# One DiT layer on one core: LayerNorm 1 and the first FFN products by token tiles, block 3 of the output projection folded into the residual in two parts, gate sums loaded behind the conditioning

## The chip, the cores and the metric

The kernel runs on one core of a Trainium2 chip. The metric is the device time of one execution in microseconds (us); smaller is better. The engines are TensorE (PE in the profile, its weight loads PEld), VectorE (DVE), ScalarE (ACT), GpSimd (POOL) and SyncE (SP), which issues the DMA transfers. All weights are read from HBM once.

## The reference

One layer of a diffusion transformer, batch 1: 256 latent tokens `x` and 256 context tokens `ctx` of width D = 2048, and a conditioning vector `c`. All in float32.

```python
m = silu(c) @ w_ada + b_ada                # 6 modulations of width D: shift, scale, gate; shift, scale, gate
u = x * (1 + scale1) + shift1              # the context likewise, with its own vector
q, k, v = split(u @ w_in)                  # 16 query heads of 128, in two groups with 2 key heads each
o = attention(q, k, v)                     # group A: window of 128, sink; group B: RMS-normalised q, k; both rotary
x = layer_norm1(alpha * x + gate1 * (o @ w_out))
u2 = x * (1 + scale2) + shift2
h = silu(u2 @ w_gate) * (u2 @ w_up)        # hidden width 5632
x = layer_norm2(alpha * x + gate2 * (h @ w_down))
```

Each layer norm has its own weight and bias over the width.

## The kernel before

**Products.** The 256 latent tokens are two token tiles (`t`) of 128, one tile on the 128 partitions. A float32 product is made of three passes on PE in a faster format: each operand is split into `hi`, a rounded copy, and `lo`, the rest, and `mm3` (L221 to L223) adds hi by hi, hi by lo, and lo by hi into one accumulator bank `acc` of 128x512. Weights come in raw tiles of 1 MB (4 by 128 rows, 512 columns) into the rooms `raw` (4) and `araw` (2); ACT copies `hi` and DVE subtracts to get `lo`, two of 128x1024 for each raw tile (L439 and L442 while the planner below works, L211 and L212 in the FFN). A raw tile feeds 24 products, 12 for each token tile.

**Order.** Up to the first layer norm each piece of work is a step (engine, estimated duration, what it follows, rooms it takes and gives back, a due time `F.at`) of a planner, `Flow`. `Flow.run` goes through time with these estimates: on each engine the step that is ready and due first is started, and the instructions are written out in the order in which the steps started. The estimates set the order; on the chip each engine works its list through in that order, waiting where it must. SP's list of loads is made in the same way, so a load that has to wait for a room holds up those behind it. After `F.run()` the order is that of the program text.

**Stages.** 1. Conditioning columns: w_ada for the first modulation, products on PE (L476). 2. `u` and the combined projection w_in. 3. Attention in four groups of heads `gi`: scores, row maxima on DVE (L814), exponentials on ACT (L826), transposes of the probabilities on PE (L844), products with the values (L855). 4. The output projection: four blocks `n` of 512 columns, each in two halves: head groups 0 and 1 are multiplied during attention and the partial sums kept in `outacc`; head groups 2 and 3 follow after attention (`flow_out((2, 3), n, n == 3)`). Block 3 goes by token tiles: all products of tile 0, then all of tile 1. DVE adds the halves (L1020), multiplies by the gate (L1024), adds alpha times x into `xt` (L1025) and takes the statistics (L1026), per tile. 5. Layer norm 1, its scalars on DVE for each tile (`ln_scalars`, L959 to L969) and `normalise` (L976) for each of four blocks of columns; its weight and bias and the second modulation are folded into columns `mA` and `mB`. `z_part(kk)` transposes two blocks of 128 columns of `xt` for both tiles (L1215); ACT applies `mA` and `mB` (`uf`, L1219) and rounds (`u2h`, L1221), DVE subtracts (`u2l`, L1222). 6. The FFN by hidden blocks `f` of 512 columns, gate and up products, then w_down, then layer norm 2.

**Sums on DVE.** Three modulations are not computed on PE: w_ada tiles are multiplied by the conditioning and summed on DVE (`flow_vector`, L329): gate 1 into `g1b` (16 loads of 1 MB), then the first block of the second shift and scale into `adav`. When the gate's sums are there, PE adds over the partitions and spreads to all rows (`rows_of_gate`, L339, four blocks of 512); the columns of the second modulation are made likewise (`m0_columns`, L908). A second block of shifts is summed on PE (`m1_sums`, L1161), copied by ACT (`m1_copy`) and placed as columns (L1177, L1180). The rest of the second modulation (`scales`, `side`) is summed on DVE between the first FFN products.

**Spills.** As the second modulation isn't complete when the FFN starts, the first `SPLIT_F` hidden blocks are begun with the first k-groups of u2 (one group for the first `ONE_F` = 3 blocks, two for the others); ACT copies the partial sums to `spill` (L1280) and DVE adds them later.

**Warm-up.** `warm` issues small products whose results nobody reads (L1038): 8 before the first flips and 6 between the two `z_part`.

## Time and profile before

| | us |
|---|---|
| three runs | 1183.93, 1187.5, 1189.0 (median 1187.5) |
| profiled execution | 1195.69 |
| its span | 1193.9 |
| PE busy | 1159.9 (97%) |
| DVE busy | 817.2 (68%) |
| ACT busy | 531.3 (45%) |
| mean granted clock of PE | 0.988 |
| moved by DMA | 292.95 MB, mean 245 GB/s |

The profile's page gives for each engine the time in which it had an instruction, and its share of the span. A matmul of 128x512 is put down with 0.39 us, but one starts every 0.23 us where nothing is waited for, since they overlap; so idle time of PE is where none is in flight. A granted clock of 0.5 means that PE ran at half speed there. The three runs are of the same kernel without the profiler.

### The profile page before, as it was taken

To read this page: it belongs to the slowest core of one execution; us is meant where nothing else is said; L and a number is where in the kernel's file an instruction comes from. 1 tells how busy PE (TensorE), PEld (TensorE's weight loads), DVE (VectorE), ACT (ScalarE), POOL (GpSimd) and SP (SyncE) were. 2 spreads that over 40 slices of the span, in tenths; PEclk is the share of its full clock that TensorE was granted. 3 is DMA by queue.
4 is the path that set the end of the run, shared out by engine and by line. 5 is a ranking of instruction groups with operands and counts; after the bars stand their busy time and mean duration, and the time that the engine had idled before them with its cause. 6 is when DMAs were issued, how large, how long until landed. Compare 5 with 4: busy or idle time off the path is not lost.

```text
span 1193.9 us, 14384 instructions
## 1 busy us (share of the span) xinstructions
PE 1159.9 (97%) x5591; PEld 937.1 (78%) x5591; DVE 817.2 (68%) x1052; ACT 531.3 (45%) x746; POOL 24.4 (2%) x44
## 2 busy tenths in 40 slices
PE   8999899999999999999999999999999999999994
PEld 8766578787878877788888888888888888888883
DVE  4653479989887888777676566564545768676556
ACT  3331352677666245444644444444444434343340
POOL 1000200000000000010000000000000000000000
PEclk9989999999999989999999999999999999999997
DMA  8998996634677369999776565556565889777531
GB/s 275 374 382 313 383 396 240 219 112 153 233 250 245 106 240 340 351 333 337 262 216 210 181 197 186 177 185 203 177 198 191 315 312 317 289 258 247 207 133 71
DMA packets 150716, 292.95 MB, mean 245 GB/s; under 512 B 5580, under 2 KB 20332, under 8 KB 148343
## 3 DMA queue, kind: packets, MB, share of 16 engines
q1 hardware_dynamic: 150648, 292.04, 70.5%
q8 instruction: 44, 0.72, 0.2%
q14 instruction: 24, 0.20, 0.0%
HBM read 289.92 MB, written 2.10 MB: 245 GB/s over the span
## 4 chain that ended last, share of the span: by engine, by line
PE 80%; DVE 8%; DMA 8%; ACT 2%; issue 1%; POOL 0%; SPq 0%; DVEq 0%; ACTq 0%; POOLq 0%
PE acc L222 23%; PE acc L223 23%; PE acc L221 23%; DMA raw<-in_w_ada_dram 3%; DMA raw<-in_w_in_dram 3%; DVE adav L329 2%; PE wk L855 2%; DVE lo L212 1%; PE wk L476 1%; PE acc L1038 1%; DMA lgb<-in_ln_b_dram 1%; PE wk L1259 1%; PE wk L844 1%; PE wk L339 1%; DMA raw<-in_w_gate_dram 1%
## 5 line engine op out<-in xcount | busy, mean ns | idle before, releaser
L212 DVE TENSOR_TENSOR lo<-raw,hi 128x1024 fp32r<-128x1024 f32 x262 | 317.8, 1223 | 215.3 <-ACT hi L211 211.7
L211 ACT CAST hi<-raw 128x1024 fp32r<-128x1024 f32 x262 | 273.5, 1053 | 363.8 <-PE acc L223 306.9
L222 PE MATMUL acc<-lo,u2h 128*128 128x512 f32 x704 | 275.6, 391 | 1.6 <-DVE lo L212 1.6
L221 PE MATMUL acc<-hi,u2h 128*128 128x512 f32 x704 | 274.3, 392 | 1.1 <-ACT hi L211 1.1
L223 PE MATMUL acc<-hi,u2l 128*128 128x512 f32 x704 | 274.6, 390 | 0.0
L222 PEld LDWEIGHTS acc<-lo,u2h 128*128 128x128 f32 x704 | 132.6, 188 | 31.7 <-DVE lo L212 4.7
L221 PEld LDWEIGHTS acc<-hi,u2h 128*128 128x128 f32 x704 | 132.5, 188 | 28.5 <-ACT hi L211 1.5
L223 PEld LDWEIGHTS acc<-hi,u2l 128*128 128x128 f32 x704 | 132.5, 188 | 27.4
L439 ACT CAST hi<-raw 128x1024 fp32r<-128x1024 f32 (+1 forms) x82 | 83.6, 1030 | 143.3 <-PE acc L223 74.7
L221 PE MATMUL acc<-hi,hTh 128*128 128x512 f32 x344 | 135.5, 394 | 0.0
L223 PE MATMUL acc<-hi,hTl 128*128 128x512 f32 x344 | 134.0, 390 | 0.0
L222 PE MATMUL acc<-lo,hTh 128*128 128x512 f32 x344 | 134.0, 390 | 0.0
L329 DVE SCALAR_TENSOR_TENSOR adav<-raw,cs,adav 128x512 f32<-128x512 f32 (+1 forms) x128 | 121.4, 948 | 13.2 <-DMA raw<-in_w_ada_dram 11.0
L442 DVE TENSOR_TENSOR lo<-raw,hi 128x1024 fp32r<-128x1024 f32 (+1 forms) x82 | 97.5, 1195 | 37.0 <-ACT hi L439 36.7
L221 PE MATMUL acc<-hi,uh 128*128 128x512 f32 x256 | 103.8, 406 | 2.7 <-ACT hi L439 2.6
L222 PE MATMUL acc<-lo,uh 128*128 128x512 f32 x256 | 101.1, 395 | 2.8 <-DVE lo L442 2.8
L223 PE MATMUL acc<-hi,ul 128*128 128x512 f32 x256 | 100.5, 393 | 0.0
L222 PEld LDWEIGHTS acc<-lo,hTh 128*128 128x128 f32 x344 | 64.6, 188 | 14.3 <-issue 1.0
L221 PEld LDWEIGHTS acc<-hi,hTh 128*128 128x128 f32 x344 | 64.6, 188 | 14.3 <-issue 1.0
L223 PEld LDWEIGHTS acc<-hi,hTl 128*128 128x128 f32 x344 | 64.6, 188 | 13.2
L221 PEld LDWEIGHTS acc<-hi,uh 128*128 128x128 f32 x256 | 48.4, 189 | 20.0 <-ACT hi L439 6.2
L222 PEld LDWEIGHTS acc<-lo,uh 128*128 128x128 f32 x256 | 48.6, 190 | 13.6 <-DVE lo L442 4.4
(193 smaller groups left out, 1167.3 us busy)
## 6 DMA issues: line engine op xcount, KB each, us to landing
raw<-in_w_ada_dram SPq DMA_DIRECT2D x72, 1024.0 KB, 7.5
raw<-in_w_gate_dram SPq DMA_DIRECT2D x44, 1024.0 KB, 5.7
raw<-in_w_up_dram SPq DMA_DIRECT2D x44, 1024.0 KB, 5.2
raw<-in_w_down_dram SPq DMA_DIRECT2D x44, 1024.0 KB, 5.3
raw<-in_w_ada_dram SPq DMA_DIRECT2D x48, 512.0 KB, 5.8
raw<-in_w_in_dram SPq DMA_DIRECT2D x18, 1024.0 KB, 8.6
raw<-in_w_out_dram SPq DMA_DIRECT2D x16, 1024.0 KB, 5.0
raw<-in_w_in_dram SPq DMA_DIRECT2D x10, 512.0 KB, 7.5
```

The source lines that it names most:

```text
L211: nc.scalar.copy(hi[:, :n], raw[:, s : s + n])
L212: nc.vector.tensor_tensor(lo[:, :n], raw[:, s : s + n], hi[:, :n].bitcast(F32), op=ALU.subtract)
L221: nc.tensor.matmul(ps, lhsT=xh, rhs=w[0], start=first, stop=False)
L222: nc.tensor.matmul(ps, lhsT=xh, rhs=w[1], start=False, stop=False)
L223: nc.tensor.matmul(ps, lhsT=xl, rhs=w[0], start=False, stop=last)
L329: nc.vector.scalar_tensor_tensor(a[:, c : c + piece], raw[:, f : f + piece], cs[:, g * (G4 * NB // w) + j, 2:3], a[:, c : c + piece], op0= ...
L339: nc.tensor.matmul(ps, lhsT=ones, rhs=sb[:, s : s + NB], start=True, stop=True)
L439: nc.scalar.copy(hl.hi[:, :n], raw.t[:, s : s + n])
L442: nc.vector.tensor_tensor(hl.lo[:, :n], raw.t[:, s : s + n], hl.hi[:, :n].bitcast(F32), op=ALU.subtract)
L476: nc.tensor.matmul(bank.t[32 * j : 32 * j + 32, :width], lhsT=cs[:, k, 2 - 2 * i : 34 - 2 * i], rhs=raw.t[:, c * width : (c + 1) * width], ...
L844: nc.tensor.transpose(ps.t[:, k * P : (k + 1) * P], probs[i].t[:, k * P : (k + 1) * P], ident)
L855: nc.tensor.matmul(o_ps.t[:, : 2 * P], lhsT=v, rhs=pT.t[:, k].rearrange("p h q -> p (h q)"), start=k == 0, stop=k == 3)
```

## The change

1. **Loads.** A step `start` without duration on SP follows the last conditioning load of stage 1; the constants' loads (`const_loads`: rotary tables, norm weights, sinks), the gate sums' bias and their 16 loads wait for it in the plan. In the plan a `raw` or `araw` room comes back 1300 ns after its last reader (`AGAIN`) instead of 90 to 270.
2. **Gate rows and columns.** The steps `rows_of_gate`, `ln_flip` and `m0_columns` are planned 2.5 us behind their sums (`SLACK`), and the loads of the gate's sums are spread until END + 10 instead of END - 15, END being the planned end of attention.
3. **Block 3 of the output projection.** Its `hi` and `lo` take rooms of another pool (`spare`: `b4`) and are loaded 14 us earlier; the rooms `hl` are so free for the first w_gate and w_up tiles, whose loads and casts become steps of the plan (`first_gate`, `first_up`). `finish` is now single steps: for block 3 the half in `outacc` is multiplied by the gate and added to alpha times x before the products end; behind them come gate (L1035), last addition (L1041) and statistics (L1044).
4. **m1 sums.** Their loads may use `araw` too and are due 35 us earlier; `m1_copy` moves behind the first products.
5. **Layer norm 1 by token tiles.** The plan ends with the scalars and flips of tile 0 (`z_flip`, L1233). Then the program goes: `z_rest` of tile 0, scalars of tile 1, gate products of tile 0, flips of tile 1, up products of tile 0, `z_rest` of tile 1, both products of tile 1, spills. The 14 warm-up products are gone.
6. **Spills.** `SPLIT_F` is 10 instead of 8.

```diff
-SPLIT_F = 8
+SPLIT_F = 10
+SLACK = 2500
+AHEAD = 14
+    AGAIN = 1300
...
-                            heapq.heappush(back, (end + self.OTHER[e], b.pool))
+                            heapq.heappush(back, (end + (self.AGAIN if b.pool.endswith("raw") else self.OTHER[e]), b.pool))
...
-        last = F.add("SP", 500 * len(starts), lambda: first_bias(a, starts, width), [last])
+        last = F.add("SP", 500 * len(starts), lambda: first_bias(a, starts, width), [last, start])
...
-            ld = F.add("SP", dma_ns(P * G4 * NB * 4, 2048), load, take=[room])
+            ld = F.add("SP", dma_ns(P * G4 * NB * 4, 2048), load, [start], take=[room])
...
+            if gs[-1] < 3:
+                outs[n, t] = steps([ends[t], outs[n, t]], add, give=[ps])
+            elif by_tile:
+                at, F.at = F.at, F.at - 6
+                early = steps([outs[n, t], gates[n]], lambda: gate(lambda: outacc[n, t]), base)
+                F.at = at
+                outs[n, t] = steps([ends[t], early], lambda: gate(lambda: ps.t), last, spread, give=[ps])
+            else:
+                a = steps([ends[t], outs[n, t]], add, give=[ps])
+                outs[n, t] = steps([a, gates[n]], lambda: gate(lambda: outacc[n, t]), base, spread)
...
-    a = F.add("SP", 2500, const_loads)
+    a = F.add("SP", 2500, const_loads, [start])
...
-            a = F.add("PE", 900, fn, [last_sum], [room])
+            a = F.add("PE", 900, fn, [(last_sum, -SLACK)], [room])
...
-    gates = rows_of_gate(flow_vector((2 * D,), D, g1b, (gate_from, END - 15)))
+    gates = rows_of_gate(flow_vector((2 * D,), D, g1b, (gate_from, END + 10)))
...
-        F.at = END + 60
-        raw, ld = flow_load(w_ada, g * 4, 4, 3 * D + NB, NB, W)
+        F.at = END + 25
+        raw, ld = flow_load(w_ada, g * 4, 4, 3 * D + NB, NB)
+        ld.after, ld.left = [(m0_sum, 2400)], 1
+        F.at = END + 45
...
-    for t in range(NT):
-        F.add("DVE", 3300, lambda t=t: scalars(t), [outs[n, t] for n in range(4)])
+    first_gate = flow_weights(w_gate, 0, G4, 0, NB, W)
+    first_up = flow_weights(w_up, 0, G4, 0, NB, W)
+    F.at = END + 33
+    a = F.add("DVE", 3300, lambda: scalars(0), [outs[n, 0] for n in range(4)])
+    zroom = [Buf("wk"), Buf("wk")]
+    for i in range(2):
+        F.add("PE", 210, lambda i=i: z_flip(0, 2 * i), [a], [zroom[i]])
     F.run()
...
-    z_part(0)
-    warm(wps, 6)
-    z_part(2)
+    for kk in (0, 2):
+        z_rest(0, kk)
+    scalars(1)
+    first_products(0, 0)
+    for kk in (0, 2):
+        z_flip(1, kk)
+    first_products(1, 0)
+    for kk in (0, 2):
+        z_rest(1, kk)
+    adav1 = vector_sums(NB)
+    nc.scalar.copy(adav1, bank1.t)
+    for i in range(2):
+        first_products(i, 1)
+    for i in range(2):
+        for t in range(NT):
+            nc.scalar.copy(spills[0][i][:, t, :], firsts[i][t])
```

The lines move by 3 to 40: L221 to L223 are L224 to L226 in the changed kernel, L329 is L332, L339 L342, L442 L449, L908 L918, L959 to L969 are L969 to L979, L976 L986, L1161 L1200. What stands where, before and now, at three places:

**SP's loads around the constants.** Before (g1b's bias and the five loads behind it are the constants' group):

```order
L421 DMA raw<-in_w_ada_dram 128x4x512 x6
L542 DMA cxt<-in_ctx_dram 128x2x512
L312 DMA g1b<-in_b_ada_dram 1x2048
L367 DMA cosA<-in_rope_cos_dram 128x2x128
L368 DMA sinA<-in_rope_sin_dram 128x2x128
L369 DMA gq<-in_q_norm_g_dram 128x128
L370 DMA gk<-in_k_norm_g_dram 128x128
L371 DMA sinkb<-in_sink_logit_dram 128x8
L421 DMA raw<-in_w_in_dram 128x4x512
```

Now, behind the last of the conditioning loads (L424 from in_w_ada_dram), with the first gate loads (L322) next:

```order
L424 DMA raw<-in_w_ada_dram 128x4x512 x2
L424 DMA raw<-in_w_in_dram 128x4x512 x3
L315 DMA g1b<-in_b_ada_dram 1x2048
L370 DMA cosA<-in_rope_cos_dram 128x2x128
L371 DMA sinA<-in_rope_sin_dram 128x2x128
L372 DMA gq<-in_q_norm_g_dram 128x128
L373 DMA gk<-in_k_norm_g_dram 128x128
L374 DMA sinkb<-in_sink_logit_dram 128x8
L322 DMA raw<-in_w_ada_dram 128x2048 x2
```

The six small loads went behind four more w_ada loads and five more w_in loads.

**PE's gate rows.** Before, late in attention, two of the four among output products and these two between the flips of the probabilities:

```order
L223 MATMUL acc_3219<-hi_3078,oTl_2479 128x512
L844 MATMUL wk_3266<-ident_70,pr_3227 128x128 x4
L844 MATMUL wk_3273<-ident_70,pr_3230 128x128 x4
L339 MATMUL wk_3280<-g1b_131,ones_98 128x512
L339 MATMUL wk_3287<-g1b_131,ones_98 128x512
L855 MATMUL wk_3292<-pT_3278,kvacc_129 128x256 x2
L855 MATMUL wk_3292<-pT_3278,kvacc_130 128x256 x2
```

Now, behind the second half of block 0 (its last product is the first row) and ahead of block 1's (oTh_2874 is head group 2):

```order
L226 MATMUL acc_3321<-hi_3274,oTl_3163 128x512
L342 MATMUL wk_3441<-g1b_131,ones_98 128x512
L342 MATMUL wk_3447<-g1b_131,ones_98 128x512
L342 MATMUL wk_3453<-g1b_131,ones_98 128x512
L342 MATMUL wk_3457<-g1b_131,ones_98 128x512
L224 MATMUL acc_3461<-hi_3351,oTh_2874 128x512
```

All four moved out of attention, and the 144 products of blocks 1 to 3 stand behind them.

**The transition into the FFN, on PE and DVE.** PE before, from the last output product:

```order
L223 MATMUL acc<-hi,oTl 128x512
L1161 MATMUL wk<-raw,cs 32x512 x16
L1038 MATMUL acc<-ident 128x128 x8
L1215 MATMUL wk<-ident,xt 128x128 x4
L1038 MATMUL acc<-ident 128x128 x6
L1215 MATMUL wk<-ident,xt 128x128 x4
L1177 MATMUL wk<-sel,adav 128x4 x4
L221 MATMUL acc<-hi,u2h 128x512
```

PE now; twelve products of tile 0 and then tile 1's four flips (L1233) follow the first of the FFN:

```order
L226 MATMUL acc<-hi,oTl 128x512
L1200 MATMUL wk<-raw,cs 32x512 x16
L1233 MATMUL wk<-ident,xt 128x128 x4
L224 MATMUL acc<-hi,u2h 128x512
L225 MATMUL acc<-lo,u2h 128x512
L226 MATMUL acc<-hi,u2l 128x512
```

The warm-up products and tile 1's flips left the place between the sums and the first product. DVE now, in the scalars of tile 1 (mv_3787, la_3791, ly_3790), with the last rows of tile 0's `z_rest` ahead:

```order
L1341 TENSOR_TENSOR u2l_3750<-uf2_3782,u2h_3749 128x2x128
L969 BN_AGGR mv_3787<-stats_77 128x2
L973 TENSOR_SCALAR lv_3789<-mv_3787 128x1
L974 TENSOR_SCALAR la_3791<-lv_3789 128x1
L975 TENSOR_SCALAR lv_3789<-lv_3789 128x1
L976 TENSOR_SCALAR ly_3790<-la_3791 128x1
L978 TENSOR_SCALAR la_3791<-ly_3790,lv_3789 128x1
L979 TENSOR_SCALAR ly_3790<-la_3791,ly_3790 128x1
```

and before, at the end of the same scalars and behind them:

```order
L969 TENSOR_SCALAR ly_3721<-la_3722,ly_3721 128x1
L976 TENSOR_SCALAR xt_76<-xt_76,mv_3718,ly_3721 128x512
L212 TENSOR_TENSOR lo_3746<-raw_3743,hi_3745 128x1024
L212 TENSOR_TENSOR lo_3750<-raw_3743,hi_3749 128x1024
L1222 TENSOR_TENSOR u2l_3759<-uf2_3787,u2h_3758 128x512
```

The scalars of tile 1 stood ahead of every `u2l`; now they stand behind tile 0's, and two of the late modulation's sums (L332) stand among their last rows, ahead of tile 1's normalise:

```order
L978 TENSOR_SCALAR la_3791<-ly_3790,lv_3789 128x1
L332 SCALAR_TENSOR_TENSOR adav_3886<-raw_3889,cs_93,adav_3886 128x512
L979 TENSOR_SCALAR ly_3790<-la_3791,ly_3790 128x1
L332 SCALAR_TENSOR_TENSOR adav_3886<-raw_3889,cs_93,adav_3886 128x512
L986 TENSOR_SCALAR xt_76<-xt_76,mv_3787,ly_3790 128x512
```

Ahead of these, tile 1's gate multiplication of block 3, which waits for the last output product, stands in front of tile 0's scalars.

## Prediction

> **What bounds the kernel now.** I read the page first, then busy time by stretches of 25 us, then the waits and timelines of the stretches in which TensorE (PE) is not full. From the page:

> ```profile
> span 1193.9 us, 14384 instructions
> PE 1159.9 (97%) x5591; PEld 937.1 (78%) x5591; DVE 817.2 (68%) x1052; ACT 531.3 (45%) x746; POOL 24.4 (2%) x44
> ```

> PE is the bound: 34.0 us without a matmul is all that scheduling can win, apart from time at half clock. The profiled execution took 1195.7 us, its span plus 1.8 us; the median of the three shown is 1187.5 us, 8.2 lower. I sum against the profile and take the same difference off the median. Under 0.5% (5.9 us) a measurement of this kernel cannot tell a change from none.

> The stretches (columns: window; its length and PE busy; PEld, DVE, ACT, POOL busy; granted clock; DMA share; GB/s), ending with two stretches at half clock:

> ```profile
> 275.00:300.00 25.00, 23.41 (x120) 18.88 (x119) 23.13 (x48) 18.66 (x43) 0.00 (x0) 1.00 0.60 207
> 350.00:375.00 25.00, 22.96 (x96) 16.93 (x95) 21.27 (x29) 15.40 (x31) 0.00 (x0) 0.93 0.72 239
> 375.00:400.00 25.00, 25.00 (x116) 20.90 (x115) 19.93 (x26) 10.39 (x13) 0.00 (x0) 1.00 0.60 203
> 450.00:475.00 25.00, 23.03 (x108) 18.40 (x107) 20.87 (x24) 13.76 (x20) 2.73 (x4) 1.00 0.92 334
> 475.00:500.00 25.00, 24.63 (x107) 19.49 (x106) 20.04 (x18) 11.81 (x14) 0.00 (x0) 1.00 1.00 352
> ...
> 355.85:359.25 3.40, 3.40 (x5) 1.44 (x5) 3.24 (x5) 3.40 (x7) 0.00 (x0) 0.50 0.87 286
> 427.55:434.35 6.80, 6.80 (x27) 6.16 (x26) 4.76 (x7) 4.63 (x8) 0.95 (x1) 0.50 1.04 403
> ```

> So there are four places: the start, the end of attention, the transition into the FFN, and the FFN's first products.

> **A. Const and gate loads behind the conditioning.** PE's stalls there, then SP's issues and the first readers of what they bring:

> ```profile
> 134.20 0.50 PE L221 MATMUL acc<-hi,uh 128*128 128x512 f32 x1 [1.69 <-ACT hi L439]
> 135.54 0.50 PE L222 MATMUL acc<-lo,uh 128*128 128x512 f32 x1 [0.83 <-DVE lo L442]
> 144.40 0.50 PE L222 MATMUL acc<-lo,uh 128*128 128x512 f32 x1 [0.65 <-DVE lo L442]
> ...
> 119.01 0.37 SPq L312 DMA_DIRECT2D g1b<-in_b_ada_dram  x1
> 127.36 0.38 SPq L421 DMA_DIRECT2D raw<-in_w_in_dram  x1
> ...
> L684 DVE TENSOR_TENSOR kvacc<-kvacc,cosA x2: 424/424/424, 183.2 to 185.7; 128x256 f32<-128x256 f32 x2
> L329 DVE SCALAR_TENSOR_TENSOR g1b<-raw,cs,g1b x32: 1272/1278/1286, 155.8 to 332.3; 128x1024 f32<-128x1024 f32 x32
> ```

> Six small issues hold SP from 119.01 to 127.36 ahead of a w_in load; they now stand behind five more w_in and four w_ada loads. The three stalls are 1.69 + 0.83 + 0.65 = 3.2 us. The last goes (its load was issued behind), and I take 0.55 off the first pair, whose casts also queue on ACT: gain 1.2, bounds 0 and 3.2. The const loads come some 27 us later (nine loads of 1 MB at the 352 GB/s of the row 475 to 500, 3.0 each) and cost nothing: the rotary tables are first read at 183.2, some 25 us after they would now be there; without that cover DVE's rotations, and PE behind them, would be late by as much as is missing of it. The gate sums start later: rival 4.

> **B. Gate rows out of attention.** PE is followed into its idle time:

> ```profile
> 355.80 2.06 PE L339 MATMUL wk<-g1b,ones 128*128 128x512 f32 x2 [2.04 <-ACT pr L826]
> ...
> 350.37 2.60 DVE L329 SCALAR_TENSOR_TENSOR adav<-raw,cs,adav 128x1024 f32<-128x1024 f32 x2 [2.10 <-DMA raw<-in_w_ada_dram]
> ...
> 354.87 0.78 ACT L826 ACTIVATE pr<-wk,nm,qsc 128x512 f32<-128x512 f32 x1 [4.98 <-DVE nm L822]
> ```

> DVE waits 2.10 for a load and sums it for 2.60 before it takes the softmax maxima; ACT waits 4.98 for these, PE 2.04 for ACT. The half clock that follows costs 3.4 x 0.5 = 1.7. The stretch 275 to 300 lacks another 25 - 23.41 = 1.59. The change takes the four rows to behind block 0's products, puts output products between scores and flips, and spreads the sums over a longer time. The rows keep their cost: they move. Bounds: 0 (the stall only shifts) to 1.59 + 2.04 + 1.7 = 5.3. The loads still land later than their sums want now and then; I take 4.2, nearer the upper end, since the new order of PE puts two lots of 12 output products (2.7 us each at 0.23) where the wait of 2.04 was.

> **C. The transition.** PE from its last output product, and the DVE and ACT steps that decide it:

> ```profile
> 418.51 3.64 PE L1161 MATMUL wk<-raw,cs 128*32 128x512 f32 x32
> 422.09 2.05 PE L1038 MATMUL acc<-ident 128*128 128x128 f32 x16
> 426.49 0.55 PE L1215 MATMUL wk<-ident,xt 128*128 128x128 f32 x3 [2.24 <-DVE xt L976]
> 426.87 2.17 PE L1038 MATMUL acc<-ident 128*128 128x128 f32 x12
> 428.83 1.06 PE L1215 MATMUL wk<-ident,xt 128*128 128x128 f32 x4
> 429.69 1.71 PE L1177 MATMUL wk<-sel,adav 128*128 128x4 f32 x8
> 431.25 0.77 PE L221 MATMUL acc<-hi,u2h 128*128 128x512 f32 x1
> 434.61 0.39 PE L223 MATMUL acc<-hi,u2l 128*128 128x512 f32 x1
> ...
> 417.45 0.26 DVE L959 BATCH_NORM_AGGREGATE mv<-stats 128x2 f32<-128x24 f32 x1
> 419.99 0.55 DVE L976 TENSOR_SCALAR xt<-xt,mv,ly 128x512 f32<-128x512 f32 x1
> 422.62 0.69 DVE L1026 BATCH_NORM_STATS2 stats<-xt 128x6 f32<-128x512 f32 x1
> 426.35 2.35 DVE L212 TENSOR_TENSOR lo<-raw,hi 128x1024 fp32r<-128x1024 f32 x2
> 437.13 0.75 DVE L329 SCALAR_TENSOR_TENSOR adav<-raw,cs,adav 128x512 f32<-128x512 f32 x1
> ...
> 427.12 1.02 ACT L1219 ACTIVATE uf<-wk,mB,mA 128x256 f32<-128x256 f32 x2 [0.33 <-issue]
> 428.17 0.62 ACT L1221 CAST u2h<-uf 128x512 fp32r<-128x512 f32 x1
> ```

> Before: 418.51 to 434.61 is 16.1 us. At full clock its work is 3.6 of sums, 8 flips and 8 small products at 0.11 (1.7, half the doubled rows) and 8 products at 0.23 (1.8): 7.1. So 9.0 us are lost, to warm-up matmuls, to the wait of 2.24, and to half clock.

> After, with M the end of the conditioning sums (E, the last output product, + 3.6): tile 0's products end 24 x 0.23 = 5.5 before E, and on DVE gate, lo, add, lo and statistics (3 x 0.7 + 2 x 1.2 = 4.5) fit. Then tile 1's gate waits for E (0.7), and only behind it stand tile 0's scalars and normalise (417.45 to 420.54: 3.1). So flips of tile 0 start at E + 3.8 = M + 0.2. Half-size casts (some 1.1, estimated as about two thirds of 1.02 + 0.62) give products from M + 1.6, to M + 1.6 + 12 x 0.23 = M + 4.3. DVE meanwhile adds and takes tile 1's statistics (1.4, to M + 1.6), waits for the second cast, subtracts twice (to M + 3.1), and then does tile 1's scalars with two sums of 0.75 in their midst: 3.1 + 1.5, less what overlaps: M + 7.5. So the flips of tile 1 idle PE from M + 4.3 to M + 7.5. PE's losses: 0.2 + 0.9 + 3.2 = 4.3, and the clock. Behind the idle time of 2.04 that ended at 355.80 there came one half-clock period of 3.4, a cost of 1.7; 3.2 of idle should do the same. Total 6.0, gain 3.0. Bounds: all but the 1.1 of the first casts gone, 7.9 gained; DVE late by its four lo's below, 4.7, with a second half-clock period, 3.4 lost. DVE has room for it: in 375 to 400 it idles 5.1 us; the four lo's that now stand ahead (2 x 2.35 = 4.7, of which before two stood behind the second normalise and two later still) take most of that. What DVE is late there is PE's idle time.

> [...]

> The gate of block 3 in two parts is one more DVE operation per tile (5 of 0.69 for 4), but three of them instead of four behind the products; it is counted above.

> **D. FFN's first products.** ACT at the stall of 467, and PE's waits from 430 to 640:

> ```profile
> 464.07 1.48 ACT L1219 ACTIVATE uf<-wk,mB,mA 128x256 f32<-128x256 f32 x3 [2.17 <-POOL mB L903]
> 467.07 0.58 ACT L1280 COPY spill<-acc 128x512 f32<-128x512 f32 x1
> ...
> PE acc L222 <- DVE lo L212: 1.6, 3, 0.9
> PE acc L221 <- ACT hi L211: 1.1, 1, 1.1
> ```

> ACT stands 2.17 behind POOL's modulation columns, the next weight cast queues behind it, and PE loses 25 - 23.03 = 1.97 in that stretch and 0.37 in the next. With first_gate and first_up already cast and ten blocks to spread the second modulation's sums over instead of eight, fewer sums fall between two lo's. Gain 2.0; bounds 0 and 1.6 + 1.1 = 2.7. The two more blocks cost 8 spill copies of 0.58 on ACT and 8 adds on DVE of about 0.69; both engines idle a third of these stretches (ACT 11.81 and DVE 20.04 of 25 in the fullest), so nothing; without cover 4.6 + 5.5 us.

> **Sum.** 1.2 + 4.2 + 3.0 + 2.0 = 10.4, less 0.4 for the longer raw-buffer turnaround that the planner now assumes, which I cannot see in a row: profile 1185.7, median **1177.5 us**.

> **Rivals.** (1) No half clock in the new gap: 1.7 better, 1175.8. For: the half-clock stretches are one and two periods of 3.4 long, and 3.2 us that fall across the border of two leave less than 2.04 in each in one case of four. Against: the row at 355.80. [...] (2) Attention's stall only shifts and D gives nothing, since loads that cause both are the same megabytes: A and C remain, 4.2, so 1183.3. For: DVE's waits there are for data, and no byte is saved. (3) Tile 1's scalars wait for a load: the two sums amid them need a bias that SP issues behind a buffer that PE's conditioning sums free only near M. If it is issued at M + 3 and takes what the median load takes,

> ```profile
> raw<-in_w_ada_dram SPq DMA_DIRECT2D x72, 1024.0 KB, 7.5
> ```

> the flips of tile 1 start near M + 12.2: 4.7 more of idle and a second half-clock period, 1.7; 3.6 of the gain is left, 1183.9. Against: the bias is 2 KB only. (4) Slower: the gate rows themselves. Before, the sums ended at 332.3 + 1.3 and PE read them at 355.8, 22 us later. Now the loads start later and are spread 25 us further, so that slack is spent; PE stands at the rows with all later products behind it, and DVE's additions behind those. Every us late is a us lost; with its half clock the kernel is slower than before from 10.0 - 1.7 = 8.3 us on. Six of the sixteen loads late by the 2.6 that their sums take are 15.6: 1177.5 + 15.6 + 1.7 = 1194.8. Against: the rows stand behind all of attention and behind block 0, so they come later too.

> **How the numbers follow.** Main case 0.42, its own range 1173 to 1182; rival 1 0.20; rival 2 0.15; rival 3 0.13; rival 4 0.10. Faster by more than 0.5% (below 1181.6): the first two, 0.62. Same: rivals 2 and 3, 0.28. Slower: rival 4, 0.10. The best bounds together are 3.2 + 5.3 + 7.9 + 2.7 = 19.1, not likely at once; the range runs from 1171 (16.5 of that) to 1190, and leaves out rival 4 and a little at each end.

> **What would show it.** A: no wait of PE near 144. B: no wait at the gate rows, clock 1.00 around 350. C: PE idle twice behind the sums, about 1 and 3 us, ended by u2h and xt; one half-clock period. D: 450 to 500 fuller by 2 us. I am wrong if PE waits at the gate rows for DVE's g1b, if tile 1's scalars wait for a DMA, or if DVE reaches tile 1's gate late.

## The result, and the profile after

The changed kernel takes 1173.17 us (median of 4 runs, 1172.63 to 1177.28); the kernel before, on the same chip, 1188.25 us (4 runs, 1183.93 to 1191.79). The ratio is 0.9882, 95% interval 0.9842 to 0.9922: 15.1 us, or 1.2%, faster. A second comparison gave 0.9879 (0.9858 to 0.9901). The prediction was 1177.5 us within 1171 to 1190.

The profiled execution is one of 1172.63 us, 23.1 below that of before. From the page after:

```profile
span 1170.9 us, 14367 instructions
PE 1144.9 (98%) x5563; PEld 928.6 (79%) x5563; DVE 822.3 (70%) x1064; ACT 537.5 (46%) x760; POOL 25.5 (2%) x44
```

PE's idle time went from 34.0 to 26.0 us, and its busy time fell by 15.0: the 28 warm-up matmuls by the first FFN products are gone, and so is time at half clock. The half clock of before is 6.83 us from 79.4, 3.41 from 355.8 and 6.83 from 427.5 (besides the tail after the last product, in both), some 8.5 us lost, by estimate half of these 17.07 us: the products from 431.83 on start every 0.43 us there, those from 434.61 on, at full clock, every 0.23. After, none. This also explains much of the distance between 23.1 by the profiles and 15.1 by the medians: the executions of before with a mean granted clock of 0.994, which leaves room for at most one period of 3.41 us besides the tail, took 1185 to 1189 us, and the profiled one, at 0.988, 1195.7.

Where the time came from, by the start of the same products in both timelines (us):

| | before | after | gained up to here |
|---|---|---|---|
| last product of the input projection | 269.78 | 262.59 | 7.2 |
| last product of the output projection | 418.20 | 404.44 | 13.8 |
| last gate or up product | 933.49 | 910.93 | 22.6 |
| last down product | 1178.10 | 1155.91 | 22.2 |

The stretches that the prediction showed, after (columns as there):

```profile
275.00:300.00 25.00, 24.54 (x123) 19.62 (x121) 21.12 (x47) 18.33 (x35) 0.00 (x0) 1.00 0.52 191
350.00:375.00 25.00, 25.00 (x114) 19.65 (x113) 23.65 (x29) 17.68 (x27) 0.00 (x0) 1.00 0.86 303
450.00:475.00 25.00, 25.00 (x112) 20.66 (x111) 20.05 (x18) 13.68 (x17) 0.00 (x0) 1.00 0.91 324
475.00:500.00 25.00, 25.00 (x112) 20.72 (x111) 18.67 (x17) 11.97 (x14) 0.00 (x0) 1.00 0.85 297
```

PE is full in three of the four and the clock is 1.00 in all. The transition on PE, then on DVE:

```profile
404.76 3.64 PE L1200 MATMUL wk<-raw,cs 128*32 128x512 f32 x32
408.61 0.66 PE L1233 MATMUL wk<-ident,xt 128*128 128x128 f32 x4 [0.21 <-DVE xt L986]
410.43 0.50 PE L224 MATMUL acc<-hi,u2h 128*128 128x512 f32 x1 [1.17 <-ACT u2h L1340]
416.20 0.63 PE L1233 MATMUL wk<-ident,xt 128*128 128x128 f32 x4 [2.72 <-DVE xt L986]
...
404.87 0.69 DVE L1035 TENSOR_TENSOR oacc<-acc,g1b 128x512 f32<-128x512 f32 x1 [1.01 <-PE acc L226]
408.01 0.55 DVE L986 TENSOR_SCALAR xt<-xt,mv,ly 128x512 f32<-128x512 f32 x1
414.06 0.75 DVE L332 SCALAR_TENSOR_TENSOR adav<-raw,cs,adav 128x512 f32<-128x512 f32 x1
414.85 0.74 DVE L332 SCALAR_TENSOR_TENSOR adav<-raw,cs,adav 128x512 f32<-128x512 f32 x1
415.51 0.54 DVE L986 TENSOR_SCALAR xt<-xt,mv,ly 128x512 f32<-128x512 f32 x1
```

PE idles three times behind its conditioning sums: for tile 0's normalise, for its cast, and longest for tile 1's normalise, which stands behind two sums. DVE itself waited 1.01 for tile 1's products before it began tile 0's scalars.

### The profile page after: what moved, and what is told of

Its sections match the earlier page's. It is cut to its first block, busy times and chain, and to the rows that moved or that the text cites. A ratio compares the mean times of both kernels' runs of the same rounds, so it can differ in the third digit from the quotient of the medians.

```text
span 1170.9 us, 14367 instructions
## 1 busy us (share of the span) xinstructions
PE 1144.9 (98%) x5563; PEld 928.6 (79%) x5563; DVE 822.3 (70%) x1064; ACT 537.5 (46%) x760; POOL 25.5 (2%) x44
## 4 chain that ended last, share of the span: by engine, by line
PE 93%; DVE 4%; DMA 2%; ACT 1%; issue 0%; SPq 0%; DVEq 0%; ACTq 0%
PE acc L224 27%; PE acc L225 27%; PE acc L226 27%; PE wk L865 2%; PE wk L485 2%; PE acc L1070 1%; PE wk L854 1%; PE wk L1304 1%; PE wk L224 1%; PE wk L226 1%; PE wk L225 1%; PE wk L342 1%; DMA lgb<-in_ln_b_dram 1%; PE wk L572 1%; DVE adav L332 1%; DVE lo L215 0%
## 5 line engine op out<-in xcount | busy, mean ns | idle before, releaser
L215 DVE TENSOR_TENSOR lo<-raw,hi 128x1024 fp32r<-128x1024 f32 x258 | 313.8, 1223 | 206.0 <-ACT hi L214 202.6
L224 PE MATMUL acc<-hi,u2h 128*128 128x512 f32 x704 | 275.5, 391 | 1.2 <-ACT u2h L1340 1.2
L226 PE MATMUL acc<-hi,u2l 128*128 128x512 f32 x704 | 274.1, 389 | 0.0
L224 PEld LDWEIGHTS acc<-hi,u2h 128*128 128x128 f32 x704 | 132.2, 188 | 28.2 <-ACT u2h L1340 1.4
L226 PEld LDWEIGHTS acc<-hi,u2l 128*128 128x128 f32 x704 | 132.2, 188 | 27.7 <-DVE u2l L1341 0.2
L446 ACT CAST hi<-raw 128x1024 fp32r<-128x1024 f32 (+1 forms) x86 | 87.9, 1033 | 135.3 <-PE acc L226 68.9
L224 PE MATMUL acc<-hi,hTh 128*128 128x512 f32 x344 | 135.5, 394 | 0.0
L226 PE MATMUL acc<-hi,hTl 128*128 128x512 f32 x344 | 134.0, 390 | 0.0
L332 DVE SCALAR_TENSOR_TENSOR adav<-raw,cs,adav 128x512 f32<-128x512 f32 (+1 forms) x128 | 121.4, 948 | 9.0 <-DMA raw<-in_w_ada_dram 7.2
L449 DVE TENSOR_TENSOR lo<-raw,hi 128x1024 fp32r<-128x1024 f32 (+1 forms) x86 | 102.5, 1198 | 28.0 <-ACT hi L446 27.7
L224 PE MATMUL acc<-hi,uh 128*128 128x512 f32 x256 | 102.8, 402 | 1.0 <-ACT hi L446 1.0
L226 PE MATMUL acc<-hi,ul 128*128 128x512 f32 x256 | 99.9, 390 | 0.0
L224 PEld LDWEIGHTS acc<-hi,hTh 128*128 128x128 f32 x344 | 64.6, 188 | 14.1 <-issue 1.0
L226 PEld LDWEIGHTS acc<-hi,hTl 128*128 128x128 f32 x344 | 64.6, 188 | 13.4
L224 PEld LDWEIGHTS acc<-hi,uh 128*128 128x128 f32 x256 | 48.1, 188 | 17.7 <-issue 4.6
## 6 DMA issues: line engine op xcount, KB each, us to landing
raw<-in_w_ada_dram SPq DMA_DIRECT2D x72, 1024.0 KB, 7.0
raw<-in_w_gate_dram SPq DMA_DIRECT2D x44, 1024.0 KB, 5.2
raw<-in_w_up_dram SPq DMA_DIRECT2D x44, 1024.0 KB, 5.1
raw<-in_w_down_dram SPq DMA_DIRECT2D x44, 1024.0 KB, 5.6
raw<-in_w_in_dram SPq DMA_DIRECT2D x18, 1024.0 KB, 8.0
raw<-in_w_out_dram SPq DMA_DIRECT2D x16, 1024.0 KB, 4.9
```

The costliest lines, as they stand in the source:

```text
L215: nc.vector.tensor_tensor(lo[:, :n], raw[:, s : s + n], hi[:, :n].bitcast(F32), op=ALU.subtract)
L224: nc.tensor.matmul(ps, lhsT=xh, rhs=w[0], start=first, stop=False)
L226: nc.tensor.matmul(ps, lhsT=xl, rhs=w[0], start=False, stop=last)
L332: nc.vector.scalar_tensor_tensor(a[:, c : c + piece], raw[:, f : f + piece], cs[:, g * (G4 * NB // w) + j, 2:3], a[:, c : c + piece], op0= ...
L446: nc.scalar.copy(hl.hi[:, :n], raw.t[:, s : s + n])
L449: nc.vector.tensor_tensor(hl.lo[:, :n], raw.t[:, s : s + n], hl.hi[:, :n].bitcast(F32), op=ALU.subtract)
```

## The experiments

Each was timed against the kernel before on the same chip; ratios are to that. The changed kernel itself ran along once as the yardstick. Differences to it are of medians, and its nine executions lie between 1172.5 and 1177.3 us. Four runs (gate sums, SPLIT_F 8, three moves, AGAIN alone) were made on a second chip, where the kernel before took as long (medians 1189.3 there, 1187.4 and 1189.6 on the first). Where executions overlap with those nine, a difference of 2 or 3 us is not certain.

**The changed kernel again.**

> The changed kernel itself, again, beside the others on the same chip. Both theories: 1173 us, ratio to before near 0.988. If half-clock stretches come and go with where idle gaps fall, its executions should lie at 1172.6 to 1173.5 and now and then 3 to 5 us above.

1173.45 us (1172.52 to 1176.0), ratio 0.9879. Its profile has what the first had not, a half-clock stretch at the transition. What follows the idle stretch, in the first profile and in this one (columns as above):

```profile
416.20:419.60 3.40, 3.40 (x17) 2.90 (x18) 3.33 (x7) 2.89 (x8) 0.00 (x0) 1.00 0.28 49
```

```profile
416.40:419.80 3.40, 3.40 (x10) 2.61 (x9) 3.36 (x7) 3.13 (x8) 0.00 (x0) 0.50 0.43 122
```

The same gap, 2.72 us in one execution and 2.75 in the other, was followed by half clock in only one: 17 products start in 3.4 us in the first profile, 10 in this one. The last section shows where the two gaps lie.

**AGAIN undone.**

```diff
-    AGAIN = 1300
...
-  heapq.heappush(back, (end + (self.AGAIN if b.pool.endswith("raw") else self.OTHER[e]), b.pool))
+  heapq.heappush(back, (end + self.OTHER[e], b.pool))
```

> The changed kernel with AGAIN undone: in the plan a raw room comes back 90 to 270 ns after its last reader again. Theory: the gain up to the end of the projections (7.2 us between the two profiles) comes from AGAIN, since SP's loads are put in an order in which it no longer stands at a room that isn't free while other rooms are (before: no load issued from 90.2 to 103.1 us). Then this kernel loses about 5 us: 1178, with PE waits before 150 us again. Rival: that gain comes from the constants and gate loads standing behind the conditioning; then this kernel stays within 1.5 us of 1173.

1176.4 us (1173.59 to 1181.03), ratio 0.9902 (0.9879 to 0.9926): 3 us slower than the changed kernel by the medians, with executions that overlap (the fastest, 1173.59, is 1 us above the fastest of the changed kernel). Its profile is of the slowest execution. There all of the loss lies early: the input projection ends 9.0 us later, the last output product also 9.0, and two half-clock stretches (6.83 from 82.2, 3.41 from 136.8) make 5.1 of it. SP's rows around the hole, in the changed kernel, then with AGAIN undone, then in the kernel before:

```profile
88.14 1.24 SPq L552 DMA_DIRECT2D cxt<-in_ctx_dram  x1
95.48 0.37 SPq L424 DMA_DIRECT2D raw<-in_w_ada_dram  x1
96.73 0.37 SPq L424 DMA_DIRECT2D raw<-in_w_in_dram  x1
```

```profile
91.16 1.17 SPq L546 DMA_DIRECT2D xt<-in_x_dram  x1
105.34 0.37 SPq L423 DMA_DIRECT2D raw<-in_w_ada_dram  x1
106.20 0.37 SPq L423 DMA_DIRECT2D raw<-in_w_in_dram  x1
```

```profile
89.00 1.17 SPq L537 DMA_DIRECT2D xt<-in_x_dram  x1
103.07 0.37 SPq L421 DMA_DIRECT2D raw<-in_w_ada_dram  x1
```

With AGAIN undone no load is issued for 13 us, as in the kernel before (90.2 to 103.1); in the changed kernel for 6. In that of before the w_ada load at the head of SP's queue waits 12.4 us for PE (L476), which still reads the room, and those behind it wait too. The memory then moves less: from 100 to 110 us the changed kernel moves 405 GB/s, this one 123, that of before 206.

```profile
100.00:110.00 10.00, 10.00 (x52) 6.92 (x51) 3.65 (x4) 1.99 (x2) 0.00 (x0) 1.00 1.05 405
```

```profile
100.00:110.00 10.00, 10.00 (x61) 5.99 (x60) 4.15 (x6) 0.00 (x0) 0.00 (x0) 1.00 0.37 123
```

**AGAIN alone, in the kernel before.**

```diff
+    AGAIN = 1300
...
-  heapq.heappush(back, (end + self.OTHER[e], b.pool))
+  heapq.heappush(back, (end + (self.AGAIN if b.pool.endswith("raw") else self.OTHER[e]), b.pool))
```

> The kernel before with AGAIN alone. Theory: AGAIN by itself fills SP's hole (no load from 90.2 to 103.1 us) and with it PE's waits at 77.7 and 78.9 and the half clock behind these: 4 us without the clock, up to 7 with it: 1181 to 1184. Rival: it only helps together with start, since constants and gate loads take the same places: 1187.

1181.74 us (1180.56 to 1184.06), ratio 0.9934 (0.9908 to 0.996): 7.5 us faster than before by the medians, half of the whole change, from one number in the planner. By its profile the input projection ends 6.3 us earlier than in the profile of before, and the last output product 10.4: AGAIN alone also clears the stall at the gate rows, though these stay within attention. PE there, before and with AGAIN:

```profile
350.00:360.00 10.00, 7.96 (x25) 4.85 (x24) 8.68 (x12) 5.13 (x11) 0.00 (x0) 0.83 0.69 224
```

```profile
350.00:360.00 10.00, 10.00 (x52) 7.91 (x50) 8.38 (x12) 7.65 (x16) 0.00 (x0) 1.00 0.84 280
```

**start undone:** constants, gate bias and gate loads are planned as before.

```diff
-        last = F.add("SP", 500 * len(starts), lambda: first_bias(a, starts, width), [last, start])
+        last = F.add("SP", 500 * len(starts), lambda: first_bias(a, starts, width), [last])
...
-            ld = F.add("SP", dma_ns(P * G4 * NB * 4, 2048), load, [start], take=[room])
+            ld = F.add("SP", dma_ns(P * G4 * NB * 4, 2048), load, take=[room])
...
-    a = F.add("SP", 2500, const_loads, [start])
+    a = F.add("SP", 2500, const_loads)
...
```

> The changed kernel without the step start: constants, gate bias and gate loads are planned as before, ahead of the last conditioning loads. Theory (AGAIN gave the early gain): it loses only what the prediction put under A, 1.2 us: 1174 to 1175. Rival (start gave it): it loses some 7 us: 1180.

1176.52 us (1174.47 to 1179.78), ratio 0.9899 (0.9876 to 0.9922): 3 us slower by the medians, with executions that overlap. Neither expectation fits closely: between the two, nearer to the theory's. In the profile the wait for the weights' casts near 127 us grows and takes a half-clock stretch with it (3.41 from 130.2; a second one, from 420.3, stands behind the gap of the transition):

```profile
127.51 0.50 PE L224 MATMUL acc<-hi,uh 128*128 128x512 f32 x1 [1.94 <-ACT hi L446]
128.88 0.50 PE L225 MATMUL acc<-lo,uh 128*128 128x512 f32 x1 [0.86 <-DVE lo L449]
```

In the changed kernel these two waits are 1.0 and 0.8. With them its last output product is 4.1 us later.

**Gate sums timed as before.**

```diff
-SLACK = 2500
+SLACK = 0
...
-    gates = rows_of_gate(flow_vector((2 * D,), D, g1b, (gate_from, END + 10)))
+    gates = rows_of_gate(flow_vector((2 * D,), D, g1b, (gate_from, END - 15)))
```

> The changed kernel with the gate sums' timing of before: SLACK 0 and loads spread until END - 15. Theory: the 6.6 us gained between the projections' end and the last output product come from the gate rows leaving attention and their sums being spread; undone, PE waits for the softmax again near 340 to 350, 2 to 3 us of idle and a half clock now and then: 1176 to 1179. Rival: that gain came from the finer DVE steps (one addition at a time) and AGAIN's order of loads: 1173 to 1174.

1179.82 us (1178.38 to 1180.52), ratio 0.9916 (0.9891 to 0.9942): 6.4 slower than the changed kernel by the medians, and each of its executions is slower than all of those; a little more than expected, and not where expected. In the profile the last output product is 2.9 us later. Of these, 0.9 are there at the end of the input projection, and 2.0 are two waits for the softmax, 1.0 each at 268.8 and 272.3, not at 340 to 350. The rest is the transition: eight of the late sums, not two, now stand among tile 1's scalars. First and last of them on DVE, and PE's flips of tile 1:

```profile
413.47 0.75 DVE L332 SCALAR_TENSOR_TENSOR adav<-raw,cs,adav 128x512 f32<-128x512 f32 x1
...
419.16 0.74 DVE L332 SCALAR_TENSOR_TENSOR adav<-raw,cs,adav 128x512 f32<-128x512 f32 x1
...
420.51 1.09 PE L1233 MATMUL wk<-ident,xt 128*128 128x128 f32 x4 [5.53 <-DVE xt L986]
```

A half-clock stretch of 6.83 us from 419.2 follows. So the run doesn't measure the gate's timing alone; what it shows is the price of sums among those scalars: the flips of tile 1 wait 5.53 with eight of them and 2.72 with two.

**SPLIT_F 8.**

```diff
-SPLIT_F = 10
+SPLIT_F = 8
```

> The changed kernel with SPLIT_F 8. Theory: the 3.9 us gained in the FFN's first part come from the sums of the second modulation being spread over ten blocks; undone, PE waits for hi and lo near 450 to 540 again: 1176 to 1177. Rival: they come from gate and up tiles cast ahead of layer norm 1: 1173 to 1174.

1174.73 us (1172.71 to 1176.87), ratio 0.9875 (0.9847 to 0.9902), against 0.9879 with 10: no difference that can be measured. From 420 to 560 us PE waits 0.4 in one place. The ten blocks give nothing.

**Layer norm 1 for both tiles at once.**

```diff
-    for i in range(2):
-        F.add("PE", 210, lambda i=i: z_flip(0, 2 * i), [a], [zroom[i]])
+    F.add("DVE", 3300, lambda: scalars(1), [outs[n, 1] for n in range(4)])
     F.run()
...
+    warm(wps, 8)
...
-    for kk in (0, 2):
-        z_rest(0, kk)
-    scalars(1)
-    first_products(0, 0)
-    for kk in (0, 2):
-        z_flip(1, kk)
-    first_products(1, 0)
-    for kk in (0, 2):
-        z_rest(1, kk)
+    z_part(0)
+    warm(wps, 6)
+    z_part(2)
...
```

> The changed kernel with layer norm 1 for both tiles at once again: both tiles' scalars end the plan, then 8 warm-up products, flips of both tiles, 6 warm-up products, flips, and the first products of both tiles; the preloaded gate and up tiles, the block 3 in two parts and all else stay. Theory (the prediction's chain): DVE ends tile 1's scalars at E + 0.7 + 3.1 + 1.4 + 3.1 = E + 8.3 with E the last output product, first product near E + 10.5; now it is E + 5.8 with a second gap of 2.7 later; so 2 us slower by idle time and up to 3.4 by half clock: 1175 to 1178. Rival: the token tiles give nothing, the gain of the transition came from the preloaded tiles: 1173.

1175.71 us (1174.54 to 1177.1), ratio 0.9893 (0.9872 to 0.9914): 2.3 slower by the medians, as the chain gave it, though the intervals overlap. In this profile the first FFN product starts 11.0 us behind the last output product, against 6.0 in the changed kernel, which loses 2.7 of that again in its later gap.

**First gate and up tiles loaded behind the plan.**

```diff
-    first_gate = flow_weights(w_gate, 0, G4, 0, NB, W)
-    first_up = flow_weights(w_up, 0, G4, 0, NB, W)
...
     F.run()
+    first_gate = load_split(w_gate, 0, 0)
+    first_up = load_split(w_up, 0, 0)
...
```

> The changed kernel with the first gate and up tiles loaded and cast behind the plan, as before, instead of inside it. Theory: their four rests (4.7 us) stand among the first scalars and u2l on DVE, so products of tile 0 start late: idle at the transition grows by 2 to 4 us: 1175 to 1178; near 446 nothing changes, since ACT's order there is that of the changed kernel. Rival: the loads come in time anyway and DVE has room: 1173 to 1174.

1178.77 us (1178.06 to 1180.83), ratio 0.991 (0.9889 to 0.9932): 5.3 slower by the medians, a little more than expected, and each execution is slower than all of the changed kernel's. PE at the transition, then ACT:

```profile
414.06 0.79 PE L224 MATMUL acc<-hi,u2h 128*128 128x512 f32 x1 [5.34 <-ACT u2h L1340]
420.47 0.63 PE L1233 MATMUL wk<-ident,xt 128*128 128x128 f32 x4 [1.74 <-DVE xt L986]
...
410.88 1.99 ACT L214 CAST hi<-raw 128x1024 fp32r<-128x1024 f32 x2 [15.81 <-DMA raw<-in_w_up_dram]
```

With token tiles and without preloaded tiles the kernel is 3 us slower than the other way round: the first product waits 5.34 for tile 0's cast on ACT. That cast stands behind those of the up tile, which wait for its load; so ACT and a load delay the first product, not the rests on DVE that the theory named, and a half-clock stretch of 6.83 us from 410.8 is added. In the kernel before, only the gate tile stood there, and the up tile came later; so the 5.3 us hold more than the return to that.

**Two more projections ahead of z_part(4), in the kernel before.**

```diff
-    run(merge(first_half[1 : 2 * ONE_F - 1], scales))
+    run(merge(first_half[1 : 7], scales))
...
-    run(merge(first_half[2 * ONE_F - 1 : cutoff], side))
+    run(merge(first_half[7 : cutoff], side))
```

> The kernel before with two more of the first projections ahead of z_part(4) and z_part(6), nothing else. It tests the cause of the 2.3 us lost near 467 to 470 in the profile of before. Theory: they come from the weight cast behind POOL's wait on ACT; the stall there goes, and the kernel gains about 2 us: 1185.5 to 1186.5. Rival: the sums between two rests on DVE make PE wait whatever stands on ACT (the prediction's reason): the stall shifts, 1187 to 1189.

1193.92 us (1187.16 to 1202.5), ratio 1.0025 (0.9998 to 1.0052): no gain, so the theory failed here; the median is above the rival's 1187 to 1189 too. PE's waits from 440 to 560 us, 2.7 in the profile of before, are:

```profile
PE acc L221 <- ACT u2h L1221: 1.7, 1, 1.7
PE acc L221 <- ACT hi L211: 1.6, 1, 1.6
PE acc L222 <- DVE lo L212: 1.3, 3, 0.5
```

The cast no longer waits behind POOL, but u2's own casts come late, and later weights do. In that kernel the stall shifts.

**Three moves at the transition of the changed kernel.** Tile 1's gate step is planned behind tile 0's scalars, tile 0's flips ahead of the last conditioning sum, tile 1's flips in the middle of tile 0's up products:

```diff
...
-                outs[n, t] = steps([ends[t], early], lambda: gate(lambda: ps.t), last, spread, give=[ps])
+                fns = (lambda: gate(lambda: ps.t), last, spread)
+                if t == 0:
+                    outs[n, t] = steps([ends[t], early], *fns, give=[ps])
+                else:
+                    deferred.append(lambda a: steps([ends[t], early, a], *fns, give=[ps]))
...
     a = F.add("DVE", 3300, lambda: scalars(0), [outs[n, 0] for n in range(4)])
+    deferred[0](a)
...
+        z = F.add("PE", 210, lambda i=i: z_flip(0, 2 * i), [a], [zroom[i]])
+        m1_last.after.append((z, 0))
...
     first_products(0, 0)
+    first_products(1, 0, (0, 1))
     for kk in (0, 2):
         z_flip(1, kk)
-    first_products(1, 0)
+    first_products(1, 0, (2, 3))
```

> The changed kernel with three moves at the transition: tile 1's gate multiplication of block 3 planned behind tile 0's scalars; tile 0's flips ahead of the last conditioning sum on PE; tile 1's flips in the middle of tile 0's up products. In the profile of the changed kernel PE idles 0.2 + 1.2 + 2.7 = 4.1 us there. By the chain scalars of tile 0 end some 1 us earlier, its casts are covered by the last sum (0.9), and tile 1's flips, ready some 9 us behind E, find 12 + 6 products ahead of them: idle of about 1 us is left. Theory: 3 us faster than the changed kernel, 1170 to 1171, and no half clock there. Rival: DVE is the bound of this stretch, and what PE saves it waits for a little later: 1173.

1172.2 us (1170.12 to 1173.66), ratio 0.985 (0.9822 to 0.9879): 1.3 us faster than the changed kernel by the medians, not 3, with executions that overlap. The gaps go as expected; PE from 404 to 416.2, in the changed kernel and with the moves:

```profile
404.00:416.20 12.20, 8.10 (x53) 3.86 (x51) 9.48 (x32) 2.33 (x6) 0.52 (x1) 1.00 0.76 258
```

```profile
404.00:416.20 12.20, 11.74 (x70) 6.53 (x68) 10.46 (x33) 4.13 (x11) 0.52 (x1) 1.00 0.79 259
```

That is 3.6 us less idle time, of which 1.4 come back soon, as the row from 440 of the run with the moves shows:

```profile
440.00:450.00 10.00, 8.60 (x40) 6.63 (x38) 6.67 (x7) 7.28 (x12) 2.57 (x4) 1.00 0.81 309
```

ACT there, with the moves, then in the changed kernel:

```profile
442.69 1.48 ACT L1272 ACTIVATE uf<-wk,mB,mA 128x256 f32<-128x256 f32 x3 [3.10 <-POOL mB L913]
...
445.69 1.99 ACT L214 CAST hi<-raw 128x1024 fp32r<-128x1024 f32 x2
```

```profile
446.86 0.58 ACT L1264 ACTIVATE uf<-wk,mB,mA 128x256 f32<-128x256 f32 x1
447.32 1.06 ACT L214 CAST hi<-raw 128x1024 fp32r<-128x1024 f32 x1
448.26 0.63 ACT L1266 CAST u2h<-uf 128x512 fp32r<-128x512 f32 x1
```

With the moves ACT's order is that of the kernel before, the weight cast behind both u2h, and the stall is there again; in the changed kernel the cast stands between them, and PE has no wait.

**The same with more projections ahead of z_part(4)**, two and one:

```diff
-    run(merge(first_half[2 : 2 * ONE_F - 1], scales))
+    run(merge(first_half[2 : 7], scales))
...
-    run(merge(first_half[2 * ONE_F - 1 : cutoff], side))
+    run(merge(first_half[7 : cutoff], side))
```

> The kernel with the three moves at the transition (which ran 1172.2), and two more of the first FFN projections, which need only the first four blocks of u2, ahead of the next two z_parts. In the profile of the three moves alone PE waited 1.83 us near 446 for a cast and its rest, which stood on ACT behind the modulated columns that waited 3.1 for POOL. Theory: with two more projections (11 us of products) ahead of them the casts stand before that wait, and the 3.6 us saved at the transition stay: 1170.5. Rival: DVE and the loads bound this stretch, and the time is given back once more: 1172 to 1173.

> The same with one more projection instead of two. Theory: one lot of 24 products (5.4 us) covers POOL's 3.1 us as well: 1170.5 to 1171. Rival: 1172 to 1173.

With two 1168.13 us (1168.01 to 1171.86), ratio 0.9829 (0.9804 to 0.9853); with one 1168.82 (1168.51 to 1170.26), ratio 0.9827 (0.9801 to 0.9852). They beat the changed kernel by 5.3 and 4.6 us, more than expected, and each of their executions lies below each of its. From 405 to 560 us PE's waits are, with two:

```profile
PE wk L1238 <- DVE xt L986: 0.3, 1, 0.3
PE acc L224 <- ACT u2h L1348: 0.2, 1, 0.2
```

## Why the prediction was right, and where its steps were not

The time lay in the range and the direction was right; the gain was 15.1 us for 10.0. Right by its size, only partly by its reasons, and with luck: the sum was made for the profiled executions, and these are 23.1 us apart, not 10.0. Taking the same difference off the median was a weak step. The profiled execution of before lies 7.4 us above its median and holds more half clock than most, so it showed more to gain than an average one has. The parts below are read from the profiles, where they add up to 22 us.

**A** was the step that failed most: 1.2 forecast, 7.2 up to the end of the input projection by the profiles: 3.4 of it half clock, 3.8 waits of PE (5.5 before, 1.7 now). I looked only at 120 to 150 us and at SP's issues there, and left out the waits of 77.7 and 78.9, the half clock after them and SP's hole. The two waits in the kernel before:

```profile
77.65 0.50 PE L221 MATMUL acc<-hi,uh 128*128 128x512 f32 x1 [0.87 <-ACT hi L439]
78.91 0.50 PE L222 MATMUL acc<-lo,uh 128*128 128x512 f32 x1 [0.76 <-DVE lo L442]
```

They come before the hole, so it is not their cause. The w_in loads ahead of them were issued from 71.1 on (71.5 with AGAIN undone), in the changed kernel from 64.0 on (64.1 with AGAIN alone): the same planner setting, at another place. I charged the longer room turnaround with 0.4 as a cost. It is the strongest single part: alone it gave 7.5 us, and undoing it cost 3. That undoing costs less than it gives alone suggests that start and the other parts reach some of the same stalls. What I had put under A, start, cost about 3 us when undone and not 1.2, with executions that overlap.

**B** came to 6.6 for 4.2, but for its larger part the reason named, the gate rows' place, isn't needed: with AGAIN alone they stay in attention and PE has no stall there, and that alone gains 4.1 of the 6.6. DVE's waits for adav's loads from 200 to 380 us (total, times, longest), before and with AGAIN alone:

```profile
DVE adav L329 <- DMA raw<-in_w_ada_dram: 5.3, 3, 2.1
```

```profile
DVE adav L330 <- DMA raw<-in_w_ada_dram: 0.5, 1, 0.5
```

In the changed kernel there is none. So loads that come in time are enough to free DVE for the maxima at the gate rows. The smaller stall, that of 275 to 300, is another matter: with AGAIN alone PE still waits 1.8 for the softmax at 271.6, with the gate sums timed as before 2.0 in two waits near 270, and in the changed kernel 0.5. There the timing of the gate sums helps; how much of it the moved rows add could not be separated, since undoing them changes the transition too.

**C** was worked out step for step: waits of 0.2, 0.9 and 3.2 were forecast; 0.21, 1.17 and 2.72 came, in the order named. Of the 9.0 us lost before, 4.1 are left, 4.9 gained for 3.0; the difference is the half clock, which did not come in the first profile and did in the second, where the gain is 3.2. So rival 1 and the main case are both this kernel, from one execution to the next, and rival 1's reason, a gap that falls across the border of two periods, is what the first profile shows (last section). Undone, the preloaded tiles cost 5.3, which holds the late up tile, and the token tiles 2.3; the two can't be added up to C.

**D** gave 3.9 for 2.0, behind the transition up to the last gate or up product; PE's waits there fell from 3.3 to 0.8, and no wait shows the rest. Both its reasons fell: ten blocks for eight give nothing, and without the preloaded tiles PE has no wait from 421 to 609 us either. What the profiles show is ACT's order, with the weight cast between the two u2h: where the order of before returned, so did the stall. It is not this order alone. In the kernel before with two more projections, the cast stands between the two u2h (471.97) and the stall only moved. With the three moves and two more projections both u2h (452.5 and 453.6) stand ahead of the next cast (456.5), and PE has no wait: the casts that it needs first were done at 451.3. Why the waits went in the changed kernel stays open to that extent.

**The rivals.** Rival 2 fell with B and D. Rival 3's place was right and its mechanism wrong: the sums amid tile 1's scalars do decide, not by a load they wait for but by standing there, two in this kernel with 2.7 us of idle, eight in an experiment with 5.5. Rival 4 fell wholly. The gate's sums and its rows on PE in the changed kernel:

```profile
L332 DVE SCALAR_TENSOR_TENSOR g1b<-raw,cs,g1b x32: 1265/1279/1562, 153.1 to 341.9; 128x1024 f32<-128x1024 f32 x32
...
366.70 3.60 PE L342 MATMUL wk<-g1b,ones 128*128 128x512 f32 x8
```

Counted as in the prediction, from 341.9 + 1.3, they are 23.5 us apart, before 22.2. I had moved the sums' end by the 25 us of the plan; it moved by 9.6, and the rows by 10.9.

## What to carry to other kernels

In a queue that issues loads in a fixed order, a planner that believes buffers free too early can make the head of the queue wait and all behind it, here 13 us without a load against 6: look for stretches in which no load is issued and the memory moves less (123 and 206 GB/s here against 405), and at the order of the loads ahead of each wait for data. A chain of waits on one engine can be worked out to about half a us from rows of the profile, and what is interleaved into it must be counted. After a wait is removed, look at the next stretch of the same engines: here 1.4 of 3.6 us came back 30 us later until more products stood ahead of it. And before a sum is made against a profile, its execution should be compared with the others: here it was 7.4 us slower than the median.

## What the hardware showed that I had not expected

```profile
411.33:414.74 3.41, 2.15 (x10) 1.42 (x8) 2.94 (x13) 0.20 (x1) 0.00 (x0) 1.00 1.00 390
414.74:418.15 3.41, 1.95 (x11) 1.72 (x12) 3.34 (x7) 1.47 (x5) 0.00 (x0) 1.00 0.03 7
```

```profile
412.98:416.39 3.41, 0.67 (x6) 0.63 (x6) 3.30 (x9) 0.16 (x1) 0.00 (x0) 1.00 0.39 153
```

So the idle time by periods is 1.3 and 1.5 us in the one execution, which stayed at full clock, and 2.7 in the other, which did not. In the profile of before, at full clock and without start and tail, the periods with 1.63, 2.04 and 2.24 us of idle PE (from 75.95, 352.43 and 424.11) were followed by half clock, and those with 1.47 and 1.44 (from 130.56 and 277.34) and all with less were not. In the first profile of the changed kernel none has more than the 1.5 above, and none was followed by half clock. Why the clock follows idle time in this way was not shown.
